# Retention of the second block, two heads at a time: score products alternate between the halves of the array's rows

## The chip, the cores and the metric

The kernel runs on one core of one Trainium2 chip. The metric is device time in microseconds (us), the median of several runs of the whole program. The engines are TensorE (PE, with its weight loads as PEld), VectorE (DVE), ScalarE (ACT), GpSimd (POOL) and the queues that issue DMAs.

## The reference

One sequence of 512 tokens with 1024 features goes through two blocks. The first is a mixer (an mLSTM and a dilated attention) and sixteen routed experts. The second prepends 16 meta tokens (528 tokens in all) and has two layers, each with a mixer and a feed-forward part. The change concerns the retention heads of that second mixer:

```python
RET_HEADS, RET_DK, RET_DV = 4, 48, 96
D_MIX = RET_W + POOL_W + FOX_W               # 384 + 256 + 384
for l in range(DEPTH_2):                     # two layers
    h = hybrid_layer(h, ...)

def hybrid_layer(h, ...):
    q_r, k_r, v_r, g_r, u_p, q_f, k_f, v_f, f_logit = split(h @ w_in)
    qr, kr = rotary(q_r), rotary(k_r)
    o_r = retention(qr, kr, vr)              # o[i] = sum over j <= i of gamma**(i-j) (q_i . k_j) v_j, per head
    o_r = silu(g_r) * head_group_norm(o_r, ret_gn_g)
    o_p = multiscale_pool(u_p)               # trailing means over 2, 4, 8, 16 tokens
    o_f = forgetting_attention(q_f, k_f, v_f, log_sigmoid(f_logit + b_f))   # 6 heads of 64, causal
    h = layer_norm(ALPHA * h + concat(o_r, o_p, o_f) @ w_out)
    return layer_norm(ALPHA * h + (silu(h @ w1) * (h @ w3)) @ w2)
```

## The kernel before

Features stand on partitions and tokens along the free dimension. A dense product in float32 is done as three products of exact 12-bit parts (lines 1377 to 1379, and 1618 to 1620 for the values). Dense work is a stream of jobs, `S`: a call `S.step(us)` emits about that much of it (by its own cost numbers), and `S.until(key)` emits until that job is done. A scheduler then orders the emitted instructions for each engine: an instruction whose inputs or buffers are not there yet is passed by others that were emitted after it.

In the mixer of the second block (`mixer`, from line 1524) the units of retention, attention and pooling are generators. The main loop (line 1918) runs in rounds. In each round every active generator is advanced once, with a `step()` of 1.2 us of dense work behind each of them and one more at the end. `_pipe` starts one unit a round and advances all those that are live. Retention is active from the first round, attention (three pairs of heads, a unit for each of four query tiles, and two tail units for the last 16 tokens) joins after round 4, pooling after round 14. The output projection `wout` follows on the stream when it is empty.

`ret_unit(hd, half)` (line 1693) is one head and one part of the queries, tokens 0 to 287 or 288 to 527. Its first stage multiplies keys by queries for each key tile of 128 tokens (`s<-rqk`, line 1706: 48 rows, in rows 0 to 47 of the array for an even head and 64 to 111 for an odd one), and right behind each product DVE multiplies the scores by the decay (`sw<-s,c_gam`, line 1708). The products of the first part are 288, 160 and 32 columns wide and lie in one PSUM bank. Those of the second part are 240 and 240 in one bank, and 240, 144 and 16 in another. The second stage sums values (`o<-sw`, line 1714) and lets ACT square and copy the sums (lines 1718, 1719). The third forms the norm (lines 1722 to 1725) and, for the heads 0 to 2, calls `S.until(14)`, the last job of the gates, applies the gates (line 1731) and writes the operand of `wout`. Eight units a layer run in the order of heads 3, 0, 1, 2.

Buffers that matter here: PSUM tiles of the kind `s` have four banks, `o` two and `d` (dense) two. SBUF work tiles (`wk`: `sw`, `gv`, `gx`, the attention's `lg` and `PT`, and others) share eight slots. `x3` is a fixed place for the sums of head 3, and `gx` holds those of another head over both of its parts.

The attention's `unit` (line 1769) already works on two heads at once, whose score products (`s<-fqk`, line 1777, 64 rows each) lie in different halves of the array's rows and are emitted one behind the other.

Of the kernel before, what the change touches and what calls it, by code (L numbers as in the profile page):

```python
# [13 lines left out]
AF = mybir.ActivationFunctionType  # L14
OP = mybir.AluOpType
# [17 lines left out]
VSUB, PMUL, VAFF = (1, 3, 5, 7), (2, 4, 6), (1, 5)  # feature tiles of the last norm by engine: DVE subtracts, Pool multiplies, DVE shifts  # L33
# [6 lines left out]
# ---------------------------------------------------------------- host layout  # L40

def _fm(w):
    """[K, M] -> [M/128, 128, K/128 * 128]: stationary tiles, input features on partitions."""
    k, m = w.shape
    return np.ascontiguousarray(
        w.reshape(k // 128, 128, m // 128, 128).transpose(2, 1, 0, 3)).reshape(m // 128, 128, k)


def _padcols(w, groups, width):
    """Columns of w taken group by group, each placed at the start of a band of `width`."""  # L50
    out = np.zeros((w.shape[0], len(groups) * width), np.float32)
# [48 lines left out]
def _host(inp):  # L100
# [88 lines left out]
    # tables that depend on shapes alone  # L189
# [45 lines left out]
# ---------------------------------------------------------------- the program  # L235
# [9 lines left out]
class _Job:  # L245
# [11 lines left out]
    def prep(self, whole=True):  # L257
        """the rest of the preparation, or one step of it"""
# [12 lines left out]
class _Stream:  # L271
    """Dense products in the order of their emission. A job is prepared in two steps, the load of its weights
    (for the next `deep` jobs) and their split (`lead` us ahead). Its run yields the tensor engine's time in us, or None
    while it cannot go on; what has to wait for another engine goes to a tail."""
# [5 lines left out]
    def add(self, key, prep, run, cost=5.0, slow=0):  # L280
        """slow: the time between the steps of a preparation that goes along with the jobs before it"""
        self.jobs.append(_Job(key if isinstance(key, list) else [key], prep, run, cost, slow))
# [22 lines left out]
    def tail(self, g, job=None):  # L305
        """goes on with the steps of g, each after as much time as the one before it yields"""
# [16 lines left out]
    def _one(self):  # L323
        """emits one piece, returns its cost in us"""
# [30 lines left out]
    def until(self, key, flush=False):  # L355
        """goes on until the job is done; flush: its tails at once"""
# [13 lines left out]
    def weave(self, g, first, us):  # L370
        """the rest of the jobs, a step of g after each `us`"""
# [7 lines left out]
def _pipe(units):  # L379
    """the stages of the units, one behind the other"""  # L380
# [12 lines left out]
class _K:  # L393
# [16 lines left out]
    # -- exact split of float32 into two parts of 12 bits  # L410
    def split_w(self, w, n, at=None):
        """w: [128, n] SBUF -> (hi, lo); at: pool, tag, columns and slots"""
# [9 lines left out]
    def after(self, ins, prev):  # L422
        """ins goes behind prev on their engine"""
# [8 lines left out]
    # -- whole program  # L432
# [38 lines left out]
    # -- helpers of the first block  # L471
    def rsqrt(self, r, x, scale, eps, c=1.0, tmp=None):
        """r = c * (scale * x + eps) ** -0.5, the engine's value with one step of Newton's method; r may not be x"""
# [14 lines left out]
    # -- first block, up to the residual after the mixer  # L488
    def first_mixer(self, ctx, mid, keep):
# [32 lines left out]
        # modulation rows: four partial sums side by side, each over a quarter of a half of the features  # L522
# [42 lines left out]
        # first norm  # L565
# [17 lines left out]
        # projections: gates, recurrent input, output gate, then queries, keys and values of the attention  # L583
# [5 lines left out]
        def dense(m, ev, *a):  # L589
# [22 lines left out]
            # the first tile in two parts: the second half of the input is complete later  # L612
# [72 lines left out]
        def ev_qk(ps, i, n):  # L685
# [11 lines left out]
            # queries of a tile stand in reverse, so that their relative positions run up along the partitions  # L697
# [33 lines left out]
        # relative position terms  # L731
# [45 lines left out]
        # modulated input  # L777
# [11 lines left out]
        # recurrent mixer, both directions in quadratic form; units of one head and one query tile  # L789
# [13 lines left out]
        def rec_unit(g, t):  # L803
# [8 lines left out]
            # forward key tiles 0..t, then backward key tiles t..3  # L812
# [58 lines left out]
        # dilated attention: one softmax over the union of the patterns, each key counted as often as it occurs  # L871
# [92 lines left out]
        def square(m, r):  # L964
            """second norm, once the tokens are complete; the router's products are taken before it"""
# [7 lines left out]
            if m == 7:  # L973
                # logits with the tokens on partitions
# [64 lines left out]
        # output projection and residual by halves of the tokens; second norm and router go along  # L1039
# [4 lines left out]
    # -- expert choice  # L1044
    def router(self, ctx):
# [23 lines left out]
        # tokens on partitions, for the gather  # L1069
# [7 lines left out]
        # the largest 64 of each expert, eight at a time  # L1077
# [9 lines left out]
        # slots from 1 on, 0 for a token that the expert leaves out; tokens on partitions, then experts on partitions  # L1087
# [16 lines left out]
    # -- routed experts  # L1104
# [3 lines left out]
    def experts(self, ctx):  # L1108
# [6 lines left out]
        # weights come in pieces of 1 MB; two of them first take places that other tiles need later  # L1115
# [17 lines left out]
        def hold():  # L1133
            """what stands in the two places later on: results and gates of two experts; sums, inputs of two experts"""
# [5 lines left out]
        def gather(p, c):  # L1140
            """inputs of experts 2p and 2p + 1, as exact one-hot products; half c of the features"""
# [56 lines left out]
        def down_last(hds, gu, og):  # L1198
            """features 256 c to 256 c + 255 of the last expert, which complete h; the statistics of the norm that follows"""
# [48 lines left out]
        def onehot(e):  # L1248
            """gate weight of each token at the slot that it has with the expert"""
# [27 lines left out]
        # downward products follow one step behind; those of the last expert come after all of its upward ones  # L1277
# [24 lines left out]
    # -- second block: tokens are the 16 meta tokens and the 512 of the sequence; dense products go by halves  # L1302
# [64 lines left out]
    def mmh(self, ps, r, ks, X, order=None, part=None, cut=None):  # L1367
        """ps[:, 0:n] = W^T x for the tokens r; ks: (split piece, column tile in it, k, rows). Yields its cost in us.
        order: the k-tiles that are ready, in the order of their use. part: first or second part of the sum, cut: its range."""
# [12 lines left out]
    def mmk(self, pss, r, ws, X):  # L1382
        """the same for several column tiles at once, each feature tile of x for all of them before the next one"""
# [17 lines left out]
    def stat(self, k, r):  # L1401
        """running sums over feature tiles of h and of its square"""
# [20 lines left out]
    def norm(self, g, b, r, X, keep=True):  # L1423
        """layer norm of the tokens r of h, in steps; keep: also in the place of h"""
# [42 lines left out]
    def pair(self, ws, n=1024, at=None):  # L1467
        """loads and splits one or two weight tiles of n columns"""
# [5 lines left out]
    def halves_of(self, name, l, R, ws, n, run, cost, at={}, head=None):  # L1474
        """jobs for the eight feature tiles by pairs, first for one half of the tokens, then for the other half, which
        begins with the weights that are still there; head: job for the first three tiles of the first half"""
# [24 lines left out]
    def wout(self, l, R, M, order):  # L1501
# [10 lines left out]
        def head(kept):  # L1512
            """the products of the feature tiles of M that are there go ahead of the last ones"""
# [10 lines left out]
    def mixer(self, l, X, ln, RO, mp):  # L1524
# [43 lines left out]
        # operands of the retention heads, rotated; the forget gates ride along in rows 48 to 53 of the first tile  # L1568
# [32 lines left out]
        # values, tokens on partitions, in the place of h  # L1601
# [28 lines left out]
        # output gates of the retention heads  # L1630
# [22 lines left out]
        # multi-scale pooling  # L1653
# [35 lines left out]
        # retention, quadratic form, queries in two parts; the values are centered, so the sums have no mean  # L1689
        cuts = [slice(0, 288), slice(288, L2)]  # L1690
        gx = {}

        def ret_unit(hd, half):
            i, o = divmod(hd, 2)
            o = slice(64 * o, 64 * o + 48)
            q, k = qk[2 * i], qk[2 * i + 1]
            c = cuts[half]
            n = c.stop - c.start
            banks = [[0, 1, 2]] if half == 0 else [[0, 1], [2, 3, 4]]
            sws = {}  # L1700
            for js in banks:
                ps, sw, at = self.sps(), self.wk("sw"), 0
                for j in js:
                    a = max(c.start, 128 * j)
                    w, kp = c.stop - a, nt[j]
                    nc.tensor.matmul(ps[:kp, at:at + w], k[o, tsl[j]], q[o, a:c.stop], start=True, stop=True)
                    sws[j] = sw[:kp, at:at + w]
                    nc.vector.tensor_mul(sws[j], ps[:kp, at:at + w], cst["c_gam"][:kp, hd, a - 128 * j:c.stop - 128 * j])
                    at += w
            yield  # L1710
            po = self.ops()
            for j in sws:
                a = max(c.start, 128 * j) - c.start
                nc.tensor.matmul(po[:96, a:n], VT[:nt[j], j, 96 * hd:96 * hd + 96], sws[j], start=(j == 0), stop=(j == len(sws) - 1))
            if half == 0:
                gx[hd] = x3 if hd == 3 else self.wk("gx")[:, :L2]
            x, v = gx[hd][:96, c], self.wk("gv")[:96, :n]
            nc.scalar.activation(v, po[:96, :n], AF.Square)
# [417 lines left out]
```

## Time and profile before

| what | value |
| --- | --- |
| time, median of 3 runs | 2672.7 us (2671.11 to 2677.9) |
| profiled execution, first to last instruction | 2671.3 us |
| TensorE busy | 2561.6 us (96%) |
| VectorE, ScalarE, GpSimd busy | 1308.1, 849.1, 370.0 us |
| mean granted TensorE clock | 0.982 |

The profiled execution has no time of its own beside its span. The median of the runs is 1.4 us above that span. The first block and the experts take the span up to about 1340 us. The retention of the first layer runs from about 1419 to 1523 us, that of the second layer from about 2074 to 2178 us.

### The profile page before, as it was taken

Reading aid. Unit: us, or ns where it says so; the run is one execution under the profiler, and the core shown is the slowest. Engines: PE = TensorE matmul, PEld = TensorE weight load, DVE = VectorE, ACT = ScalarE, POOL = GpSimd, SP = SyncE. Lnnn points to the kernel's source line nnn. Section 1 sums busy time; section 2 is a strip of 40 time slices with the busy share of each in tenths; the row PEclk is TensorE's granted clock in tenths of the full one; section 3 lists DMA queues with packets and bytes.
Section 4 is the critical chain, followed back from the end, with each engine's and each line's share of the span. In section 5 each row is a group of like instructions: output and inputs, shape, how many; then the busy total and the mean of one; then the engine's idle time right before and its main releaser. Section 6 shows DMA issues by size and latency. Waiting matters only on the chain.

```text
span 2671.3 us, 39752 instructions
## 1 busy us (share of the span) xinstructions
PE 2561.6 (96%) x16400; PEld 1822.5 (68%) x16400; DVE 1308.1 (49%) x2483; ACT 849.1 (32%) x1601; POOL 370.0 (14%) x361
## 2 busy tenths in 40 slices
PE   7999989999999999999989998999999999899997
PEld 4777765333343433333478878999999888899997
DVE  5476750101010110101273568878876447978796
ACT  3455541000001010000133435434443434534344
POOL 0000010000000000000040125112223013511123
PEclk9999989999999999999989999999999999999999
DMA  7522459999999999999922112223332211232332
GB/s 306 192 93 96 166 196 384 420 402 419 419 419 420 420 420 419 420 419 419 379 86 90 45 57 81 93 95 102 105 109 94 88 46 56 95 103 88 102 108 73
DMA packets 104673, 570.93 MB, mean 214 GB/s; under 512 B 11598, under 2 KB 14926, under 8 KB 50988
## 3 DMA queue, kind: packets, MB, share of 16 engines
q1 hardware_dynamic: 101148, 561.45, 53.4%
q10 hardware_dynamic: 3344, 6.94, 0.8%
q8 instruction: 129, 2.11, 0.3%
q14 instruction: 52, 0.43, 0.0%
HBM read 566.19 MB, written 2.16 MB: 213 GB/s over the span
## 4 chain that ended last, share of the span: by engine, by line
PE 82%; DVE 12%; ACT 2%; DMA 2%; issue 1%; POOL 1%; DVEq 0%; ACTq 0%; POOLq 0%
PE gu L1171 18%; PE py L1195 8%; PE d L1377 6%; PE d L1379 6%; PE d L1378 6%; PE s L1985 5%; PE s L1987 5%; PE s L1986 5%; PE sc L1266 3%; PE sc L1154 3%; DVE wlo L416 2%; PE gt L1182 1%; DVE qlo L1462 1%; DMA ring<-in_w 1%; PE d L1618 1%; PE d L1619 1%
## 5 line engine op out<-in xcount | busy, mean ns | idle before, releaser
L416 DVE TENSOR_TENSOR wlo<-ring,whi 128x1024 fp32r<-128x1024 f32 (+2 forms) x253 | 305.3, 1210 | 126.2 <-ACT whi L416 125.7
L416 ACT ACTIVATE whi<-ring 128x1024 fp32r<-128x1024 f32 (+2 forms) x253 | 248.7, 989 | 354.3 <-PE d L1378 130.7
L1186 DVE TENSOR_TENSOR hd<-sg,gt 128x256 f32<-128x256 f32 x64 | 27.0, 422 | 640.9 <-ACT sg L1184 640.9
L1377 PE MATMUL d<-phi,whi 128*128 128x264 f32 (+1 forms) x888 | 254.4, 287 | 10.5 <-DVE h L1399 7.3
L1378 PE MATMUL d<-plo,whi 128*128 128x264 f32 (+1 forms) x888 | 251.0, 283 | 0.2
L1379 PE MATMUL d<-phi,wlo 128*128 128x264 f32 (+1 forms) x888 | 250.6, 282 | 0.0
L1171 PE MATMUL gu<-ew,xin 128*64 128x512 f32 x1008 | 247.8, 595 | 0.0
L1171 PE MATMUL gu<-ew,late 128*64 128x512 f32 x1024 | 247.4, 595 | 0.0
L1195 PE MATMUL py<-ew,hd 128*64 128x512 f32 x960 | 242.3, 599 | 0.0
L1173 ACT ACTIVATE gus<-gu 128x512 f32<-128x512 f32 x64 | 38.2, 597 | 486.5 <-PE gu L1171 486.5
L1171 PEld LDWEIGHTS gu<-ew,late 128*64 128x64 f32 x1024 | 75.2, 137 | 152.5 <-issue 148.2
L1377 PEld LDWEIGHTS d<-phi,whi 128*128 128x128 f32 x888 | 166.7, 188 | 17.8 <-issue 11.9
L1171 PEld LDWEIGHTS gu<-ew,xin 128*64 128x64 f32 x1008 | 81.7, 137 | 140.4 <-issue 128.6
L1378 PEld LDWEIGHTS d<-plo,whi 128*128 128x128 f32 x888 | 167.3, 188 | 1.4 <-DVE plo L430 0.6
L1379 PEld LDWEIGHTS d<-phi,wlo 128*128 128x128 f32 x888 | 167.2, 188 | 0.2 <-issue 0.2
L1377 PE MATMUL d<-qhi,whi 128*128 128x264 f32 (+1 forms) x496 | 151.9, 306 | 2.3 <-ACT qhi L1461 1.8
L1195 PEld LDWEIGHTS py<-ew,hd 128*64 128x64 f32 x960 | 69.9, 136 | 118.4 <-issue 112.4
L1378 PE MATMUL d<-qlo,whi 128*128 128x264 f32 (+1 forms) x496 | 146.8, 296 | 1.5 <-DVE qlo L1462 1.5
L1379 PE MATMUL d<-qhi,wlo 128*128 128x264 f32 (+1 forms) x496 | 146.8, 296 | 0.0
L1225 POOL TENSOR_TENSOR late<-h 128x528 f32<-128x528 f32 x1 | 1.3, 1315 | 946.7 <-ACT late L1223 946.7
L2010 POOL TENSOR_TENSOR ring<-ring 128x512 f32<-128x512 f32 x38 | 59.3, 1560 | 441.9 <-DVE glo L416 425.3
L1377 PEld LDWEIGHTS d<-qhi,whi 128*128 128x128 f32 x496 | 97.8, 197 | 14.1 <-issue 3.9
(492 smaller groups left out, 5950.4 us busy)
## 6 DMA issues: line engine op xcount, KB each, us to landing
ew<-in_wg SPq DMA_DIRECT2D x127, 1024.0 KB, 17.3
ew<-in_wu SPq DMA_DIRECT2D x127, 1024.0 KB, 16.1
ew<-in_wd SPq DMA_DIRECT2D x120, 1024.0 KB, 17.3
ring<-in_w SPq DMA_DIRECT2D x44, 1024.0 KB, 4.9
ring<-in_win SPq DMA_DIRECT2D x22, 1024.0 KB, 4.9
ring<-in_wada SPq DMA_DIRECT2D x21, 1024.0 KB, 6.2
ring<-in_wout SPq DMA_DIRECT2D x16, 1024.0 KB, 5.0
ring<-in_w SPq DMA_DIRECT2D x24, 640.0 KB, 3.9
```

Source lines behind the costliest of these rows:

```text
L416: both = (nc.scalar.activation(hi[:, :n], w, AF.Copy), nc.vector.tensor_sub(lo[:, :n], w, hi[:, :n].bitcast(F32)))
L1154: nc.tensor.matmul(ps[:, j], self.tok[:, t, 128 * k:128 * k + 128], oh[:, t].rearrange("p a b -> p (a b)"), start=(t == 0), stop=(t == 3))
L1171: nc.tensor.matmul(ps[64 * j:64 * j + 64], x, ws[k // 4][j][:, o], start=(k == 0), stop=(k == 7))
L1195: nc.tensor.matmul(py[64 * c:64 * c + 64], hd[:, j], wd[j // 2][:, o:o + 512], start=(n == 0 and j == 0), stop=(n == 3 and j == 3))
L1266: nc.tensor.matmul(ps, ys[e][s, 128 * (k % 4):128 * (k % 4) + 128], ogs[e][s], start=(i == 0), stop=(i == len(es) - 1))
L1377: nc.tensor.matmul(ps[:, :n], a, X[0][:p, k, r], start=(i == 0 and part != 1), stop=False)
L1378: nc.tensor.matmul(ps[:, :n], a, X[1][:p, k, r], start=False, stop=False)
L1379: nc.tensor.matmul(ps[:, :n], b, X[0][:p, k, r], start=False, stop=(i == len(ks) - 1 and part != 0))
L1985: nc.tensor.matmul(ps, a, x[0][:, k], start=(k == 0), stop=False)
L1986: nc.tensor.matmul(ps, a, x[1][:, k], start=False, stop=False)
L1987: nc.tensor.matmul(ps, b, x[0][:, k], start=False, stop=(k == 3))
L2010: nc.gpsimd.tensor_sub(a11, a21, a11)
```

## The change

A unit is now a pair of heads (3 and 2, then 1 and 0) and one part of the queries, so there are four units a layer. For each bank group the score products of the two heads are emitted alternately, each head into a bank of its own, and all of the decay multiplications come behind all the products of the group. The second part of the queries has a yield behind each of its two groups, the value sums have a yield behind each head, and the norms of both heads share the last stage. `gx` is taken anew for each part. The numbers and shapes of the instructions are the same. The rest of the diff takes out comments.

```diff
-        def ret_unit(hd, half):
-            i, o = divmod(hd, 2)
-            o = slice(64 * o, 64 * o + 48)
-            q, k = qk[2 * i], qk[2 * i + 1]
+        def ret_unit(pr, half):
+            q, k = qk[2 * pr], qk[2 * pr + 1]
             c = cuts[half]
             n = c.stop - c.start
-            banks = [[0, 1, 2]] if half == 0 else [[0, 1], [2, 3, 4]]
-            sws = {}
-            for js in banks:
-                ps, sw, at = self.sps(), self.wk("sw"), 0
+            hds = (2 * pr + 1, 2 * pr)
+            sws = {hd: {} for hd in hds}
+            for js in [[0, 1, 2]] if half == 0 else [[0, 1], [2, 3, 4]]:
+                ps, sw, at = [self.sps() for _ in hds], [self.wk("sw") for _ in hds], 0
+                todo = []
                 for j in js:
                     a = max(c.start, 128 * j)
                     w, kp = c.stop - a, nt[j]
-                    nc.tensor.matmul(ps[:kp, at:at + w], k[o, tsl[j]], q[o, a:c.stop], start=True, stop=True)
-                    sws[j] = sw[:kp, at:at + w]
-                    nc.vector.tensor_mul(sws[j], ps[:kp, at:at + w], cst["c_gam"][:kp, hd, a - 128 * j:c.stop - 128 * j])
+                    for hd, p, s_ in zip(hds, ps, sw):
+                        o = slice(64 * (hd % 2), 64 * (hd % 2) + 48)
+                        nc.tensor.matmul(p[:kp, at:at + w], k[o, tsl[j]], q[o, a:c.stop], start=True, stop=True)
+                        sws[hd][j] = s_[:kp, at:at + w]
+                        todo.append((hd, j, p[:kp, at:at + w], cst["c_gam"][:kp, hd, a - 128 * j:c.stop - 128 * j]))
                     at += w
-            yield
-            po = self.ops()
...
+                for hd, j, p, gam in todo:
+                    nc.vector.tensor_mul(sws[hd][j], p, gam)
+                yield
+            xs, vs = {}, {}
+            for hd in hds:
+                po = self.ops()
+                for j in sws[hd]:
+                    a = max(c.start, 128 * j) - c.start
+                    nc.tensor.matmul(po[:96, a:n], VT[:nt[j], j, 96 * hd:96 * hd + 96], sws[hd][j],
+                                     start=(j == 0), stop=(j == len(sws[hd]) - 1))
+                xs[hd] = x3[:, c] if hd == 3 else self.wk("gx")[:, :n]
+                vs[hd] = self.wk("gv")[:96, :n]
+                nc.scalar.activation(vs[hd], po[:96, :n], AF.Square)
+                nc.scalar.activation(xs[hd][:96], po[:96, :n], AF.Copy)
+                yield
+            for hd in hds:
+                v, x = vs[hd], xs[hd]
...
+                if hd < 3:
+                    S.until(14)
...
             yield
@@
-            for hd in (3, 0, 1, 2):
+            for pr in (1, 0):
                 for half in range(2):
-                    yield ret_unit(hd, half)
+                    yield ret_unit(pr, half)
```

## Rows read from the trace of the kernel before

**Rows 1.** The page, part 1: busy time, share and instructions of each engine.

```profile
PE 2561.6 (96%) x16400; PEld 1822.5 (68%) x16400; DVE 1308.1 (49%) x2483; ACT 849.1 (32%) x1601; POOL 370.0 (14%) x361
```

**Rows 2.** Busy time by stage: length, PE, PEld, DVE, ACT, POOL, granted clock, DMA.

```profile
1419.00:1446.00 27.00, 27.00 (x166) 21.70 (x165) 10.65 (x26) 8.21 (x18) 0.00 (x0) 1.00 0.22 79
...
1510.00:1560.00 50.00, 50.00 (x388) 41.27 (x388) 21.45 (x69) 18.13 (x45) 7.25 (x14) 0.93 0.12 43
...
1535.20:1542.00 6.80, 6.80 (x20) 4.37 (x20) 2.86 (x11) 1.89 (x5) 0.92 (x2) 0.50 0.00 0
...
1580.00:1592.00 12.00, 9.28 (x58) 6.81 (x59) 8.53 (x28) 4.84 (x14) 1.93 (x3) 1.00 0.01 1
...
2190.60:2197.40 6.80, 6.80 (x20) 4.41 (x20) 2.75 (x11) 1.89 (x5) 0.91 (x2) 0.50 0.00 0
```

**Rows 3.** Groups by line, 1415 to 1510 us (first layer): busy, mean ns, idle before.

```profile
L1706 PE MATMUL s<-rqk 48*128 48x240 f32 (+5 forms) x64 | 16.4, 347 | 0.0
...
L1714 PE MATMUL o<-sw,h 128*96 128x240 f32 (+5 forms) x64 | 12.2, 321 | 0.0
...
L1708 DVE TENSOR_TENSOR sw<-s,c_gam 128x240 f32<-128x240 f32 (+5 forms) x32 | 10.2, 328 | 12.5 <-PE s L1706 12.4
```

**Rows 4.** Timeline, head 3, first part: start, length, engine, instruction.

```profile
1418.76 0.28 PE L1619 MATMUL d<-wlo,qhi 128*16 128x256 f32 x1
...
1418.87 0.28 PE L1620 MATMUL d<-whi,qlo 128*16 128x256 f32 x1
...
1419.08 0.75 PE L1706 MATMUL s<-rqk 48*128 48x288 f32 x2
...
1419.76 0.39 PE L1377 MATMUL d<-qhi,whi 128*128 128x264 f32 x1
...
1420.53 0.43 DVE L1708 TENSOR_TENSOR sw<-s,c_gam 128x288 f32<-128x288 f32 x1
...
1421.29 0.54 PE L1706 MATMUL s<-rqk 48*128 48x160 f32 x2
...
1421.75 0.39 PE L1379 MATMUL d<-qhi,wlo 128*128 128x264 f32 x1
...
1424.01 0.41 PE L1706 MATMUL s<-rqk 48*128 48x32 f32 x2
...
1424.34 0.51 PE L1714 MATMUL o<-sw,h 128*96 128x160 f32 x2
```

**Rows 5.** Timeline, head 3, second part; below, the layer's last score product.

```profile
1424.78 0.29 PEld L1706 LDWEIGHTS s<-rqk 48*128 48x128 f32 x2 [0.20 <-issue]
1424.78 0.67 PE L1706 MATMUL s<-rqk 48*128 48x240 f32 x2
1425.38 0.24 PEld L1714 LDWEIGHTS o<-sw,h 128*96 128x96 f32 x2 [0.30 <-issue]
...
1501.77 0.21 PE L1706 MATMUL s<-rqk 48*16 48x16 f32 x2
1501.91 0.39 PE L1378 MATMUL d<-qlo,whi 128*128 128x264 f32 x1
```

**Rows 6.** Timeline of PE: the attention's score products, alone and in pairs.

```profile
1466.76 1.13 PE L1777 MATMUL s<-fqk 64*128 64x512 f32 x4
1467.81 0.39 PE L1618 MATMUL d<-whi,qhi 128*128 128x256 f32 x1
...
1478.30 0.91 PE L1777 MATMUL s<-fqk 64*128 64x384 f32 x3
...
1500.30 0.48 PE L1777 MATMUL s<-fqk 64*128 64x128 f32 x2
1500.72 0.39 PE L1377 MATMUL d<-qhi,whi 128*128 128x264 f32 x1
...
1550.25 0.49 PE L1777 MATMUL s<-fqk 64*128 64x128 f32 x4
1550.67 0.39 PE L1377 MATMUL d<-qhi,whi 128*128 128x264 f32 x1
```

More of the change, by code (lines that the diff above doesn't have):

```diff
@@ L1690, in mixer @@
         cuts = [slice(0, 288), slice(288, L2)]
-        gx = {}
-        def ret_unit(hd, half):
-            i, o = divmod(hd, 2)
-            o = slice(64 * o, 64 * o + 48)
-            q, k = qk[2 * i], qk[2 * i + 1]
+        def ret_unit(pr, half):
+            q, k = qk[2 * pr], qk[2 * pr + 1]
             c = cuts[half]
             n = c.stop - c.start
-            banks = [[0, 1, 2]] if half == 0 else [[0, 1], [2, 3, 4]]
-            sws = {}
-            for js in banks:
-                ps, sw, at = self.sps(), self.wk("sw"), 0
+            hds = (2 * pr + 1, 2 * pr)
[3 more added lines that the diff above has]
+                todo = []
                 for j in js:
@@ L1705, in ret_unit @@
                     w, kp = c.stop - a, nt[j]
-                    nc.tensor.matmul(ps[:kp, at:at + w], k[o, tsl[j]], q[o, a:c.stop], start=True, stop=True)
-                    sws[j] = sw[:kp, at:at + w]
-                    nc.vector.tensor_mul(sws[j], ps[:kp, at:at + w], cst["c_gam"][:kp, hd, a - 128 * j:c.stop - 128 * j])
-                    at += w
-            yield
-            po = self.ops()
-            for j in sws:
-                a = max(c.start, 128 * j) - c.start
-                nc.tensor.matmul(po[:96, a:n], VT[:nt[j], j, 96 * hd:96 * hd + 96], sws[j], start=(j == 0), stop=(j == len(sws) - 1))
@@ L1715, in ret_unit @@
[L1715 to L1718, printed above, removed]
-            nc.scalar.activation(x, po[:96, :n], AF.Copy)
-            yield
-            pm = self.sps()[:96, :n]
-            nc.tensor.matmul(pm, ones[:96, :96], v, start=True, stop=True)
-            nc.scalar.activation(v, pm, AF.Ln, bias=self.eps5[:96], scale=1.0 / 96)
-            nc.scalar.activation(v, v, AF.Exp, scale=-0.5)
@@ L1725, in ret_unit @@
-            nc.vector.tensor_mul(x, x, v)
-            if hd < 3:
-                S.until(14)
-                x = gx[hd][:, c]
-                nc.vector.tensor_copy(x[96:], x3[32 * hd:32 * hd + 32, c])
-                nc.vector.scalar_tensor_tensor(x, x, self.col(f"gn{l}", hd), graw[hd][:, c], op0=OP.mult, op1=OP.mult)
-                self.split_x(M[0][:, hd, c], M[1][:, hd, c], x)
-                if half:
-                    order.append(hd)
+                    for hd, p, s_ in zip(hds, ps, sw):
[3 more added lines that the diff above has]
+                        todo.append((hd, j, p[:kp, at:at + w], cst["c_gam"][:kp, hd, a - 128 * j:c.stop - 128 * j]))
@@ new lines, in ret_unit @@
+            for hd in hds:
+                v, x = vs[hd], xs[hd]
+                pm = self.sps()[:96, :n]
+                nc.tensor.matmul(pm, ones[:96, :96], v, start=True, stop=True)
+                nc.scalar.activation(v, pm, AF.Ln, bias=self.eps5[:96], scale=1.0 / 96)
+                nc.scalar.activation(v, v, AF.Exp, scale=-0.5)
+                nc.vector.tensor_mul(x[:96], x[:96], v)
+                if hd < 3:
+                    S.until(14)
+                    nc.vector.tensor_copy(x[96:], x3[32 * hd:32 * hd + 32, c])
+                    nc.vector.scalar_tensor_tensor(x, x, self.col(f"gn{l}", hd), graw[hd][:, c], op0=OP.mult, op1=OP.mult)
+                    self.split_x(M[0][:, hd, c], M[1][:, hd, c], x)
+                    if half:
+                        order.append(hd)
```

## Prediction

> **What bounds the kernel now.** I read the page first: TensorE is busy for 2561.6 of 2671.3 us, no other engine for half of the span [rows 1]. That is an average, so I read the busy time by stage over the two mixers that the change touches. In the stretch of the first retention units TensorE is busy for 27.00 of 27.00 us and VectorE for 10.65. From 1510 to 1560 it is 50.00 of 50.00 and 21.45 [rows 2]. Whenever a product of retention or attention has to wait, dense products fill TensorE. Only at the very end of the mixer, from 1580 to 1592 us, does TensorE idle, for 2.7 of 12 us [rows 2]. So TensorE time taken out of the retention shortens the mixer by as much, as long as dense work is left to fill the waits, and a wait that delays retention or attention costs nothing until that end.
>
> Then I read the groups by line for what the retention takes of TensorE: the score products of a layer 16.4 us in 64 records (32 products, each two records), the value sums 12.2 us, and the decay multiplications 10.2 us of VectorE [rows 3]. Last, the timeline for what one score product costs from its start to the start of the next instruction. In that stretch the products are spread among dense ones, in 27 runs of one or two adjacent products, from 1419.08 to 1501.77 us [rows 4, 5].
>
> **Why they are spread.** The first product of 288 columns starts at 1419.08, its multiplication on VectorE at 1420.53, and the second product, into the same bank, only at 1421.29, after that multiplication has read [rows 4]. In between stand dense products. The change emits all products of a group before any multiplication, so this wait is gone and the products of a group can stand side by side.
>
> **The price of the score products before.** The 288 columns take 1419.08 to 1419.76, 0.68 us; the 160 columns 0.46; the 32 columns 0.33 [rows 4]. The difference of the first two is 1.7 ns a column, and about 0.2 us remains that a run pays once for getting in and out. A product of 240 columns alone takes 1424.78 to 1425.38, 0.60 us, which agrees, and one of 16 takes 0.14 [rows 5]. For a layer: a record overlaps the next instruction by 0.07 us (0.75 of length against 0.68), 27 runs have 1.9 us of that, so 16.4 - 1.9 = 14.5 us [rows 3, 4]. Besides, dense products start 0.11 us apart, but the first score product starts 0.21 after the dense one ahead of it [rows 4]: 0.10 us for each of the 14 runs that follow a dense product (counted in the timeline).
>
> **The price of a pair.** The trace of before doesn't show a retention pair, but it shows the same thing in the attention. One product of 128 columns of one head alone takes 1500.30 to 1500.72, 0.42 us. Two adjacent ones, of both heads in opposite row halves, take 1550.25 to 1550.67, also 0.42 us. A pair of 512 columns takes 1.05 us [rows 6], which by 0.2 us and 1.7 ns a column is the price of a single one. So an adjacent pair costs as much as one product.
>
> The bounds for a layer, for two pairs of heads. (a) Each pair of products pays the full single price: first part 0.68 + 0.46 + 0.33 = 1.47; second part 3 x 0.60 + 0.44 (144 columns at 0.2 + 1.7 ns each) + 0.14 = 2.38; together 3.85, twice is 7.7 us. (b) The pairs of a group also follow each other without loss, 0.2 us once a group: 480, 480 and 400 columns give 1.0 + 1.0 + 0.9 = 2.9, twice is 5.8 us. (c) No overlap at all, only clusters: 960, 960 and 800 columns, 1.8 + 1.8 + 1.55, twice is 10.3 us. (d) The scheduler tears every pair apart: 14.5 us as now.
>
> I take (a). What speaks against (b) is the weight loads: a product has two, and the two loads of a product of 240 columns take 0.29 us [rows 5], so two heads at once want about 0.5 us of loads for 0.40 us of columns, and more for the narrow products.
>
> The Trainium skill, "TensorE: Matmul & The Clock Gate", section "LDWEIGHTS (loading the stationary operand)", says that a load's time goes by its columns and not by its rows, columns divided by 1.2 in ns. The trace agrees in kind: two loads of 48 rows and 128 columns take 0.29 us [rows 5]. By that page a load is 107 ns (an estimate), so twelve loads, eight, and eight with four short ones make 1.3, 0.9 and 0.9 us, with the 0.2 us of each group 3.7 us a pair of heads and 7.4 us a layer. The saving by the page would be 0.3 us a layer more than by (a).
>
> **The sum.** Score products: 14.5 - 7.7 = 6.8 us a layer, 13.6 us for both. Runs: six a layer in place of 27, so at most 6 entries from dense work for 14, 8 x 0.10 = 0.8 us, 1.6 us for both. Together 15.2 us. The other edits I cost at nothing. The multiplications are the same 32 a layer, later by up to six products. They and the value sums behind them are covered by dense work (10.65 of 27 us busy on VectorE, rows 2). The value sums keep their columns, and their runs of three or five stay. No DMA is added or moved past another. The call of `S.until(14)` comes in round 4 in place of 5, and retention ends two rounds earlier, so two steps of 1.2 us of dense work fall behind. But attention calls for `S.until(5)` and `S.until(6)` and pooling for job 10 in the same rounds as before, and from round 15 on the two programs have emitted the same. If the dense cover were gone, each group's wait from products to value sums (about 2.2 us, six multiplications of 0.33 [rows 3]) would show: six groups a layer, 13 us. The other extreme for these edits is no loss, and I take that since TensorE has no idle stretch between 1419 and 1560 in which the cover fails [rows 2].
>
> From the profiled span, 2671.3 - 15.2 = 2656.1 us. The median of the runs shown is 1.4 us above that span, so the predicted time is 2657.5 us.
>
> **Rivals.**
> 1. *The pairs don't overlap.* The heads have 48 rows and not the attention's 64, and the scheduler may put one head's products first when only one bank is free. By (c) 4.2 us a layer is saved, with the entries 10.0 us in all: 2662.7 us. By (d) there is no gain: 2672.7. For it: the attention's two 128-column products did get torn apart once, at 1500.30, where the run has two records and not four. Against it: the pairs at 1466.76 and 1550.25 [rows 6]. Chance 0.13.
> 2. *The eight work slots make the attention late* (the other side). A retention unit now holds two `sw` for each group, two `gv` and up to two `gx`. By my count of the stages, round 5 asks for thirteen slots with the attention's two `lg`, where eight exist. VectorE and ACT then wait for slots, and behind their waiting instructions stand the attention's softmax and the weight splits. TensorE goes on with dense work, so the delay shows only at the end of the mixer, where dense work is used up and TensorE now idles 2.7 us [rows 2]. A delay that isn't caught up costs its own length. It decides from 7.6 us a layer, the whole gain. Two attention units start at 1466.76 and 1478.30 [rows 6], a round of 11.5 us, so that is two thirds of one round; a whole round in each layer would give 2657.5 + 23 = 2680 us. Against it: a slot is freed by a short chain (multiplication, sum, copy, some 2 us), so I expect delays of that size, caught up later. Chance of a partial loss of 3 to 7 us a layer (2664 to 2672 us) 0.13, of a slower kernel 0.07.
> 3. *The clock moves with the stages.* From 1535.2 to 1542 and from 2190.6 to 2197.4 us the granted clock is 0.50, the lower level of 1.2 GHz [rows 2], each time after a tail unit's run of narrow products. That costs 3.4 us of full speed twice. I keep both in the sum. The stages move by 7 us in the first layer and 15 in the second, and either stretch can vanish or another appear. If both vanish the time is 2651 us. Chance 0.12 for that side; a further stretch of the kind, 2661 us, lies inside the forecast's own range.
>
> **How the numbers follow.** The forecast (pairs overlap, 5.8 to 8.5 us a layer, 2652 to 2663 us with a clock stretch either way) has 0.55; rival 1 0.13, rival 2 0.20, rival 3 0.12. About 0.3%, 8 us, is what a measurement of this kernel can tell from no change. Faster (below 2664.7): the forecast, rival 3, most of rival 1 and a little of rival 2, 0.77. Same: 0.15. Slower: 0.08. The range 2647 to 2670 us takes in (b) with both clock stretches gone at its lower end (2 x 2.8 us and 6.8 us less would be 2646 to 2647), and at its upper end partial losses. It leaves out the torn pairs and a late attention, and holds 8 in 10.
>
> **What the changed profile would show.** The score products' group still has 64 records a layer, but six to ten runs in place of 27, and its busy time falls from 16.4 to about 8 us. If it is near 10.5 us in six runs, the pairs don't overlap; if there are still some twenty runs, they are torn. The multiplications stand behind a whole group. VectorE's waits for score products change their form, not TensorE's. If TensorE's idle time at the end of the mixer grows beyond 2.7 us by several us, the attention is late. The granted clock after the tail unit shows the third rival. The prediction is wrong if the mixer isn't bound by TensorE once the score products are paired: then the busy time falls as told and the span doesn't.

## The result, and the profile after

The kernel after takes 2643.05 us (median of 4 runs, 2639.86 to 2645.13), the kernel before beside it 2674.51 us (4 runs, 2671.11 to 2677.9). The ratio is 0.988, with a 95% interval of 0.9869 to 0.9892: 31.5 us less. I had forecast 2657.5 us and a range from 2647 to 2670. The sign was right; the time lies below the range, and the gain is about twice the 15.2 us of my sum. The profiled execution of after spans 2642.1 us, and its own time is 1.8 us above its span.

The page, part 1, after, answers to [rows 1]: TensorE has lost 29.2 us of busy time in the same 16400 instructions, as much as the spans differ by. Its weight loads have lost 14.0 us, and no other engine has changed by more than 3 us.

```profile
PE 2532.4 (96%) x16400; PEld 1808.5 (68%) x16400; DVE 1305.6 (49%) x2483; ACT 849.7 (32%) x1601; POOL 370.6 (14%) x361
```

The busy time by stage after (length, PE, PEld, DVE, ACT, POOL, granted clock, DMA) answers to [rows 2]. The first stretch begins with the first score product, the second covers later units of the attention, the third follows the tail unit's narrow products, the last is the mixer's end.

```profile
1422.60:1449.60 27.00, 27.00 (x222) 25.51 (x222) 12.10 (x31) 8.41 (x18) 0.00 (x0) 1.00 0.23 79
...
1495.00:1545.00 50.00, 49.92 (x420) 41.08 (x419) 29.56 (x102) 22.50 (x60) 8.83 (x16) 1.00 0.20 72
...
1523.60:1530.40 6.80, 6.80 (x60) 5.61 (x60) 4.29 (x13) 3.49 (x8) 2.38 (x4) 1.00 0.01 2
...
1566.00:1578.00 12.00, 9.16 (x60) 6.69 (x59) 8.60 (x27) 3.77 (x14) 2.62 (x3) 1.00 0.01 1
```

In its first 27 us TensorE is as full as before, and gets 222 records through in place of 166. At the mixer's end it idles 2.84 of 12 us, where it idled 2.72. Behind the tail unit the clock is 1.00, where [rows 2] have 0.50.

The groups by line after, 1418 to 1500 us, answer to [rows 3]; the fourth line is the weight loads of the score products.

```profile
L1719 PE MATMUL o<-sw,h 128*96 128x240 f32 (+5 forms) x64 | 12.5, 322 | 0.0
...
L1712 DVE TENSOR_TENSOR sw<-s,c_gam 128x240 f32<-128x240 f32 (+5 forms) x32 | 8.3, 321 | 11.4 <-PE o L1719 6.1 <-PE s L1707 5.2
...
L1707 PE MATMUL s<-rqk 48*128 48x240 f32 (+5 forms) x64 | 6.6, 329 | 0.0
L1707 PEld LDWEIGHTS s<-rqk 48*128 48x128 f32 (+1 forms) x64 | 4.9, 174 | 1.0 <-issue 0.2
```

The same group of weight loads in the kernel before, 1415 to 1510 us:

```profile
L1706 PEld LDWEIGHTS s<-rqk 48*128 48x128 f32 (+1 forms) x64 | 9.1, 173 | 3.7 <-issue 1.0 <-DVE sw L1708 0.5
```

A score record still lasts about as long (329 ns, before 347), but 64 of them are busy for 6.6 us in place of 16.4: two run at a time. The same holds for the loads: 174 ns each as before, 64 of them in 4.9 us in place of 9.1.

The timeline of PE after, with rows that answer to [rows 4 to 6]:

```profile
1422.59 1.17 PE L1707 MATMUL s<-rqk 48*128 48x288 f32 x12
1423.69 0.39 PE L1377 MATMUL d<-qhi,whi 128*128 128x264 f32 x1
1423.92 0.28 PE L1378 MATMUL d<-qlo,whi 128*128 128x264 f32 x1
...
1432.67 2.17 PE L1707 MATMUL s<-rqk 48*128 48x240 f32 x24
1434.77 0.39 PE L1377 MATMUL d<-qhi,whi 128*128 128x264 f32 x1
1434.99 0.29 PE L1378 MATMUL d<-qlo,whi 128*128 128x264 f32 x1
1435.12 0.29 PE L1379 MATMUL d<-qhi,wlo 128*128 128x264 f32 x1
...
1490.90 0.92 PE L1783 MATMUL s<-fqk 64*128 64x384 f32 x4
1491.74 0.43 PE L1812 MATMUL o<-PT,h 128*64 128x128 f32 x2
...
1501.55 0.49 PE L1783 MATMUL s<-fqk 64*128 64x128 f32 x4
1501.97 0.39 PE L1379 MATMUL d<-qhi,wlo 128*128 128x264 f32 x1
```

The six products of a first part (960 columns of both heads) take 1422.59 to 1423.69, 1.10 us. The twelve of two groups go through in one run, 1432.67 to 1434.77, 2.10 us. A layer has five such runs (1.10, 1.01, 2.10, 1.01 and 1.00 us, 6.2 in all) in place of 27. The first dense product behind a run also takes longer than the next: 1434.77 to 1434.99, 0.22 us, against 0.13 for the one after it. So leaving the dense stream costs 0.10 us [rows 4] and coming back costs about 0.1 us again. The attention's 128-column pair, torn before (2 records at 1500.30 in [rows 6]), stands together here (4 records).

The attention's 384-column pair was not torn before, though [rows 6] show 3 records: that view ends at 1479 us, and the fourth record starts at 1479.01. The same place in the kernel before, 1478 to 1481 us:

```profile
1478.30 1.18 PE L1777 MATMUL s<-fqk 64*128 64x384 f32 x4
1479.42 0.39 PE L1618 MATMUL d<-whi,qhi 128*128 128x256 f32 x1
```

The pair took 1478.30 to 1479.42, 1.12 us, because its second product started 0.28 us after the first; after, it takes 0.84 us. It comes 68.3 us after the first score product, where it came 59.2 us after it.

### The profile page after: what moved, and what is told of

Same layout as the page of the kernel before. It is cut to its first block, busy times and chain, and to the rows that moved or that the text cites. A ratio compares the mean times of both kernels' runs of the same rounds, so it can differ in the third digit from the quotient of the medians.

```text
span 2642.1 us, 39786 instructions
## 1 busy us (share of the span) xinstructions
PE 2532.4 (96%) x16400; PEld 1808.5 (68%) x16400; DVE 1305.6 (49%) x2483; ACT 849.7 (32%) x1601; POOL 370.6 (14%) x361
## 5 line engine op out<-in xcount | busy, mean ns | idle before, releaser
L2016 POOL TENSOR_TENSOR ring<-ring 128x512 f32<-128x512 f32 x38 | 59.2, 1559 | 441.3 <-DVE glo L416 424.8
```

The source lines that it names most:

```text
L2016: nc.gpsimd.tensor_sub(a11, a21, a11)
```

## The experiments

Each differs from after, or from before where that is said, by the edit shown. The times are medians of 4 runs unless another number stands there, the ratios are to the kernel before on the same chip (2674.2 us beside the first four, 2674.3 beside the next three, 2674.5 beside after, so times of different chips can be compared).

**Both heads of a pair in the same half of the rows.** The pairs are heads 3 and 1, then 2 and 0; the planned order stays the same.

```diff
-            hds = (2 * pr + 1, 2 * pr)
+            hds = (2 + pr, pr)
...
                     for hd, p, s_ in zip(hds, ps, sw):
+                        q, k = qk[2 * (hd // 2)], qk[2 * (hd // 2) + 1]
```

> The changed kernel with other pairs: heads 3 and 1, then 2 and 0, so that both heads of a unit lie in the same half of the array's rows; the planned order of the tensor engine is the same row by row. If the gain of the score products is overlap of the two row halves, a layer's score products rise from 6.2 us (five runs, profile of the changed kernel) to about 10.3 us (960, 960 and 800 columns one after the other, five or six runs), and the time from 2643 to about 2651 us. If the products only had to stand together and the rest of the gain is the new staging, the score products' stretch and the time stay, 2643 us.

Measured: 2657.71 us (2657.03 to 2658.63), ratio 0.9941 (0.9926 to 0.9956), 14.7 us more than after. By line, 1410 to 1512 us, score products and their weight loads, and its longest score run with a stretch of the windows that begins in the run's last microsecond:

```profile
L1707 PE MATMUL s<-rqk 48*128 48x240 f32 (+5 forms) x64 | 11.8, 327 | 0.0
...
L1707 PEld LDWEIGHTS s<-rqk 48*128 48x128 f32 (+1 forms) x64 | 9.6, 180 | 1.5 <-issue 0.2
```

```profile
1429.61 4.11 PE L1707 MATMUL s<-rqk 48*128 48x240 f32 x24
```

```profile
1432.96:1436.37 3.41, 3.41 (x17) 3.35 (x17) 0.79 (x3) 0.00 (x0) 0.00 (x0) 0.51 0.00 0
```

The score products take 11.4 us a layer, again in five runs (2.07, 1.81, 4.04, 1.81, 1.69), in place of 6.2: 10.4 us for both layers. The mean granted clock of its runs is 0.9822 against 0.9835 for after, worth 3.4 us: the low stretch at 1433 us begins at the end of the 4 us run, in both layers. 10.4 and 3.4 make 13.8 of the 14.7. The weight loads are busy for 9.6 us in place of 4.9. So the row halves do overlap, products and loads, and what clustering alone saves is 14.46 - 11.42 = 3.0 us of scores a layer.

**Head by head in a group.** The products of one head come first, then those of the other; its plan has them in that order on TensorE.

```diff
-                for j in js:
-                    a = max(c.start, 128 * j)
-                    w, kp = c.stop - a, nt[j]
-                    for hd, p, s_ in zip(hds, ps, sw):
+                for hd, p, s_ in zip(hds, ps, sw):
+                    at = 0
+                    for j in js:
+                        a = max(c.start, 128 * j)
+                        w, kp = c.stop - a, nt[j]
```

> The changed kernel with the products of one head ahead of those of the other in each group, so that they don't alternate; heads still in opposite halves. If products overlap only with a neighbour in the other half, only the last of one head and the first of the other do: about 1.75, 1.4 and 1.5 us for the three groups, 9.3 us a layer in place of 6.2, and 2649 us. If the engine looked further ahead, or if standing together is all that counts, 6.2 us and 2643 us stay.

Measured: 2651.01 us (2649.93 to 2656.25), ratio 0.9919 (0.9903 to 0.9936). By line, 1410 to 1512 us, and the timeline of the groups of a first part and of the first half of a second part:

```profile
L1708 PE MATMUL s<-rqk 48*128 48x240 f32 (+5 forms) x64 | 9.7, 329 | 0.0
```

```profile
1418.31 1.76 PE L1708 MATMUL s<-rqk 48*128 48x288 f32 x12
1420.00 0.39 PE L1377 MATMUL d<-qhi,whi 128*128 128x264 f32 x1
...
1423.99 1.09 PE L1708 MATMUL s<-rqk 48*128 48x240 f32 x8
1425.00 0.39 PE L1377 MATMUL d<-qhi,whi 128*128 128x264 f32 x1
```

The total is as expected, 9.35 us a layer, and 8.0 us over after (6.3 from the scores). How it comes about is not. The group of 240 and 240 columns for each head takes 1.01 us, no more than alternating, though its order is one head, then the other. A start in that order would put the second head's first product beside the first head's second, and the whole at 0.2 + 3 x 0.41 = 1.4 us (an estimate). The eight records start in four twos, the two of each 0.02 us apart or less. The group of 288, 160 and 32 takes 1.69, with the second head beginning beside the first head's second product, and the group of 240, 144 and 16 columns (whose last weights have 16 columns) does not overlap at all: 2 x 0.98. So alternating matters, 3.1 us a layer, but not for every group.

**Multiplications behind the products, single heads.** Kernel before, with one edit: a bank's multiplications come behind all of its products.

```diff
+                    todo.append((j, ps[:kp, at:at + w], cst["c_gam"][:kp, hd, a - 128 * j:c.stop - 128 * j]))
-                    nc.vector.tensor_mul(sws[j], ps[:kp, at:at + w], cst["c_gam"][:kp, hd, a - 128 * j:c.stop - 128 * j])
                     at += w
+                for j, p, gam in todo:
+                    nc.vector.tensor_mul(sws[j], p, gam)
```

> The kernel before, units of one head as they were, with one part of the change alone: the multiplications of a bank come behind all its products. By the price of a run (0.2 us) and 1.7 ns a column the score products of a layer fall from 14.5 to about 11.5 us in 8 to 12 runs, which with fewer entries from dense work gives 7 us: 2667 us. If the new order of emission is most of the gain, it falls well below that, towards 2650 us. A clock stretch more or less is worth 3.4 us.

Measured: 2660.48 us (2658.44 to 2667.17), ratio 0.9955 (0.994 to 0.997): 13.7 us less than before, about twice what I had expected. By line, 1410 to 1512 us:

```profile
L1707 PE MATMUL s<-rqk 48*128 48x240 f32 (+5 forms) x64 | 12.1, 323 | 0.0
```

The score products take 11.55 us a layer in 8 runs, as expected, which gives 5.8 us for both layers. The rest is outside them: the dense products of the first layer stand in 34 runs in place of 48, and by the timeline (from each start to the next) they take 114.0 us in place of 118.3. Of before's 118.3 us, 3.6 lie at the lower clock, and of these 114.0 almost nothing. With such time counted at half it is 114.0 against 116.5, so 14 fewer runs are worth 2.5 us, some 0.2 us each. This was a missing piece in my sum: a score run interrupts the dense stream, and the dense stream pays too.

**Multiplications behind each pair.** After, with the pairs alternating, but each pair's two multiplications right behind it, so that the next pair waits for them as in before.

```diff
-                for hd, j, p, gam in todo:
-                    nc.vector.tensor_mul(sws[hd][j], p, gam)
+                    for hd, jj, p, gam in todo:
+                        nc.vector.tensor_mul(sws[hd][jj], p, gam)
+                    todo = []
```

> The changed kernel with each pair's two multiplications right behind the pair, as the kernel before had them behind each product. The same bank is then read before its next product, as before, so the runs are torn: in the planned order there are about 25 runs a layer, and some pairs stand alone. Priced by runs, about 11 to 12 us of score products a layer and 2653 to 2656 us. If pairing alone, without the later multiplications, carries the gain, 7.7 us a layer (each pair at the price of one product) and 2646 us.

Measured: 2661.73 us (2654.93 to 2664.53), ratio 0.9952 (0.9936 to 0.9968), 18.7 us more than after and more than I had expected. By line, 1410 to 1512 us:

```profile
L1707 PE MATMUL s<-rqk 48*128 48x240 f32 (+5 forms) x64 | 13.2, 356 | 0.2
...
L1707 PEld LDWEIGHTS s<-rqk 48*128 48x128 f32 (+1 forms) x64 | 7.5, 177 | 4.6 <-DVE sw L1712 2.9 <-issue 0.7
```

The wait for `sw` is back on the weight loads (2.9 us), the score products stand in 19 runs and take 11.8 us a layer, and the dense products are back at 48 runs and 118.2 us (114.15 in after). Scores 11.2 us for both layers, and dense runs 2 x 4.0 us, of which up to 1.7 a layer is clock, are 15.8 to 19.2. Seen from before, alternating with this wait left in (and the new staging with it) is 12.4 us faster, the later multiplications on single heads 13.7 us: 26.1 us, where the change with both parts has 31.5. So each part carries a part of the gain, and the two nearly add up.

**Units spread over eleven rounds.** After, with an idle round behind the first pair's second part and behind the second pair's first part, so that retention does not end two rounds earlier.

```diff
                     yield ret_unit(pr, half)
+                    if (pr, half) in ((1, 1), (0, 0)):
+                        yield None
```

> The changed kernel with an empty round behind its second and its third unit, so that retention lasts eleven rounds as before the change in place of nine; the products stay paired except in the last group of a layer, which the planned order tears. The torn group costs 0.7 us a layer and two or three more runs. If the end of retention two rounds earlier is worth nothing by itself, about 2645 us. If the closer staging carries part of the gain that the score products and the clock leave open (some 4 us a layer), up to 2651 us.

Measured: 2658.49 us (2655.64 to 2660.11), ratio 0.9937 (0.9923 to 0.995). Two of four low stretches, behind the tail unit of the first layer and at the mixer's end of the second:

```profile
1522.20:1532.40 10.20, 10.20 (x36) 7.48 (x34) 3.35 (x12) 2.25 (x7) 1.64 (x3) 0.50 0.00 0
...
2222.00:2232.10 10.10, 9.58 (x35) 6.76 (x36) 3.90 (x17) 3.78 (x11) 1.46 (x2) 0.50 0.00 0
```

Its score products take 7.19 us a layer (seven runs, the last group torn in two), 2 us more for both. The mean granted clock of its runs is 0.9788 against 0.9835, and (0.9835 - 0.9788) x 2650 is 12.5 us. The two make 14.5 of the 15.4 us that it is slower than after. So the earlier end of the retention is worth nothing that shows, apart from where it leaves the clock.

**The tail unit's products set apart, in before and in after.** A foreign edit, the same in both: a yield between the four heads' narrow products of the tail unit's last stage, so that dense work comes between them.

```diff
+                if hh < nh - 1:
+                    yield
```

> The kernel before with one foreign edit: a yield between the heads of the attention's tail unit, so that its narrow products (20 of 16 columns, some 3.1 us in one piece) stand apart with dense products between them. If that piece is what lets the clock fall (0.5 for 6.8 us in both layers of the profile of before), the low stretches behind it are gone and the time falls by up to 6 us, to about 2669 us. If the clock falls for another reason, it falls again, and the time stays or rises by a us or two for the added runs.

Measured in before: 2669.15 us (11 runs, 2665.43 to 2674.18), ratio 0.9983 (0.9974 to 0.9991), 5.1 us less. The stretches in which [rows 2] show 0.50:

```profile
1536.00:1545.00 9.00, 9.00 (x85) 7.37 (x84) 3.94 (x13) 2.76 (x7) 1.19 (x3) 1.00 0.36 117
2188.00:2197.00 9.00, 9.00 (x84) 7.34 (x83) 3.98 (x13) 2.71 (x7) 1.22 (x3) 1.00 0.35 118
```

The clock is 1.00 there, and the mean over the runs is 0.9835 (before 0.9811).

> The same edit in the changed kernel, whose profile shows no low stretch there. If the changed kernel's place in time decides whether the clock falls, and it seldom falls in this kernel, nothing is gained: 2643 to 2645 us. If the clock falls in some executions of this kernel too (its runs spread from 2639.9 to 2645.1 us), the spread narrows and the median goes to about 2641 us.

Measured in after: 2641.62 us (2641.05 to 2644.52), ratio 0.9878 (0.9863 to 0.9893). This is the lowest time of all, but its interval overlaps that of after (0.9869 to 0.9892), so the two can't be told apart. Its mean clock is 0.9858. With the tail unit apart in both, the change is worth 2669.15 - 2641.62 = 27.5 us. The mean clocks of the two still differ by 0.0023 (0.9835 and 0.9858), so this difference has a part from the clock too.

**Both kernels once more, unchanged,** for the clock in another execution.

> The kernel before once more, for a second profile of it. If the clock falls behind the tail unit's narrow products whenever this kernel runs, it falls again in both layers (6.8 us at 0.50 each). If it depends on when the piece comes in an execution, it may stand at 1.00 there, and the time is then 2668 to 2671 us and not 2671 to 2678.

> The changed kernel once more. If it is free of the low stretch for a reason of its own, the clock stays at 1.00 behind the tail unit; if it was the place in time of the one profiled execution, it may fall here, in one layer or both, with 3.4 us for each. The score products stay 6.2 us a layer in five runs.

Measured: before 2673.08 us (span 2671.4), after 2645.53 us (span 2643.7). The windows of before again, then of after again, behind the tail unit of each layer:

```profile
1535.00:1541.80 6.80, 6.80 (x20) 4.41 (x21) 2.73 (x11) 1.89 (x5) 0.91 (x2) 0.50 0.00 0
2190.40:2197.10 6.70, 6.70 (x19) 4.31 (x20) 2.75 (x11) 1.90 (x5) 0.91 (x2) 0.50 0.00 0
```

```profile
1517.90:1524.60 6.70, 6.70 (x29) 5.22 (x28) 3.17 (x12) 2.15 (x6) 1.66 (x3) 0.50 0.01 2
2159.60:2166.30 6.70, 6.70 (x31) 5.22 (x32) 2.54 (x10) 1.81 (x5) 1.64 (x3) 0.50 0.00 0
```

The same kernel after, with the same narrow products, falls to the lower level in this execution and not in the one profiled first. So after again has the stretch in both layers, as the first execution of before has in [rows 2], and the two mixers can be compared at the same clock. (Before again has one low stretch more, 3.4 us from 1425.8 us on.)

## Why the prediction was wrong

**What held.** TensorE sets the time, and what is taken out of it there shortens the span. The windows of the whole stage, from the first score product to the mixer's end: before, after, and after again.

```profile
1419.00:1609.20 190.20, 186.52 (x1347) 155.50 (x1346) 100.10 (x270) 75.06 (x177) 33.03 (x48) 0.98 0.20 67
```

```profile
1422.60:1596.60 174.00, 170.92 (x1346) 147.87 (x1346) 98.35 (x270) 75.16 (x177) 33.30 (x48) 1.00 0.21 73
```

```profile
1417.30:1594.30 177.00, 173.88 (x1346) 150.16 (x1346) 98.31 (x270) 75.18 (x177) 33.66 (x48) 0.98 0.21 72
```

The stage loses 16.2 us, or 13.2 us with the low clock as before, and TensorE's busy time loses nearly as much. Pairs cost like one product, the multiplications' later place and the work slots cost nothing that shows, and the waits stay covered: TensorE idles for 3.1 us of the stage after, 3.7 before.

I summed each kind of instruction on TensorE over this stage of the first layer, each from its start to the next start (idle time counts with the instruction ahead of it):

| us, in so many runs | before | after | after again |
| --- | --- | --- | --- |
| dense products | 118.31 in 48 | 114.15 in 38 | 115.45 in 38 |
| retention's score products | 14.46 in 27 | 6.21 in 5 | 6.22 in 5 |
| attention's score products | 15.79 in 19 | 12.81 in 17 | 13.54 in 17 |
| value sums | 11.48 in 10 | 11.04 in 10 | 11.04 in 10 |
| transposes | 9.24 | 8.72 | 9.58 |
| all others | 20.86 | 21.09 | 21.23 |
| sum | 190.14 | 174.02 | 177.06 |
| of it at the lower clock | 6.83 | 0 | 6.83 |

The low stretch falls on dense and attention products in before and on transposes too in after again, and idle time hides in the rows. So here are both layers together, with idle time by itself and time at the lower clock counted at half (an estimate; by it the two executions of before agree within 0.1 us in their sum, those of after within 0.8):

| us, both layers | before | after | after again |
| --- | --- | --- | --- |
| retention's score products | 28.9 | 12.4 | 12.4 |
| dense products (95, 76, 76 runs) | 226.4 | 223.3 | 222.9 |
| attention's score products | 29.1 | 26.2 | 26.1 |
| value sums | 23.0 | 22.1 | 22.1 |
| transposes | 18.3 | 17.3 | 17.1 |
| all others | 40.3 | 40.7 | 40.5 |
| idle | 6.7 | 5.3 | 5.4 |
| sum | 372.7 | 347.4 | 346.6 |

So the mechanism held, and the terms of the sum were too small or missing.

**The step that failed first: the price of a pair, "I take (a)".** I chose (a), 7.7 us a layer, against (b), 5.8 us, because of the weight loads. The layer takes 6.2 us, the 1.0 us a group of (b), the first group 1.1. The loads of two row halves run at the same time (9.1 us busy became 4.9, same length each, and 9.6 with both heads in one half), so the reason against (b) was false. The term was 13.6 us for both layers and measured 16.5.

The figure that I had worked out from the Trainium skill's page "TensorE: Matmul & The Clock Gate", section "LDWEIGHTS (loading the stationary operand)", 7.4 us a layer, fails in the same way: it adds the loads up one behind the other, and the measured 6.2 us is less.

**The second step: the runs, "8 x 0.10 = 0.8 us".** The count of runs was nearly right (five where I said six, and only the first of them follows a dense product), but I priced only the way out of the dense stream. The way back costs as much, and every score run splits a dense run: in the first layer 48 runs became 38, in both 95 became 76. The term was 1.6 us for both layers, and the dense products lost 3.1 to 3.5 us, nearly 0.2 us for each run that is gone. Undoing the order alone (multiplications behind each pair) brings all 48 runs back.

**What I left out: the attention's own pairs, and small terms.** The attention's score products lose 2.9 to 3.0 us in both layers. In the first layer three pairs make it up, 1.4 us, and the second repeats it: the 384-column pair at 1478.30 (1.12 us became 0.84), the 128-column pair (two times 0.41 became 0.42), and a later 384-column pair, 116 us after the first score product. That one stood in two runs within the low stretch, and after it stands in one:

```profile
1535.25 1.64 PE L1777 MATMUL s<-fqk 64*128 64x384 f32 x2
...
1537.55 1.65 PE L1777 MATMUL s<-fqk 64*128 64x384 f32 x2
```

```profile
1524.54 0.92 PE L1783 MATMUL s<-fqk 64*128 64x384 f32 x4
```

That the first two gain because the retention no longer takes score banks in between is my reading of the timeline; no run isolates it. For the third it can't be: the layer's last retention score product lies 33 us ahead of it. With the tail unit set apart in both kernels only the first two are left, 0.7 us a layer. It is not the place of the multiplications: with those behind each pair the attention keeps its 17 runs. Value sums, transposes and idle time, which have no term in my sum, lose 0.9, 1.0 to 1.2 and 1.3 to 1.4 us.

**The sum at equal clock.** Scores 16.5, dense runs 3.1 to 3.5, attention 2.9 to 3.0, the small terms 3.3 to 3.4, less 0.2 to 0.4 for all others: the two mixers are 25.3 to 26.1 us shorter. I had 15.2. From the first score product to the end, before takes 1252.2 us and after again 1226.5, 25.7 us less. (Of it 1.7 us is a low stretch between the layers that only before has.)

**The clock, rival 3.** I kept both low stretches in the sum and gave their vanishing a chance of 0.12. They are no property of the kernel alone: before shows both in both executions, after shows none in one and both in the other. The mean granted clock is 0.9812 over the 22 runs of before beside the first seven experiments and 0.9835 over the four of after, and 0.0023 x 2650 is some 6 us. With the 25.7 us that makes about the 31.5 that were measured. So about 6 us of the measured gain is where the clock happens to fall, by a mean and not run by run. Four runs of after don't tell whether that is chance or the change's doing, and no experiment takes it out: with the tail unit set apart in both kernels the difference is 27.5 us, but the mean clocks are again 0.0023 apart. Without that part the time would have been some 2649 us, just inside my range, with the same terms of the sum too small.

**A slip in the range.** For its lower end I wrote 2 x 2.8 us for (b) in place of (a). By my own prices that is 2 x 1.9 us (7.7 less 5.8), and only with 1.9 do 2646 to 2647 us come out.

**Rival 1 (no overlap)** fell: without overlap the score products take 11.4 us a layer, not 6.2. **Rival 2 (attention late)** happened and cost nothing: the second attention unit is 9 us late, the next ones catch up, and TensorE's idle time at the mixer's end is 2.84 us, before 2.72. No run tried the slots by themselves.

**What stays open:** what decides, in one execution, whether the clock falls behind the tail unit, and whether it falls less often in after; and why the attention's pairs stand together more often.

## What to carry to other kernels

When a small product is put into a stream of dense ones, price the interruption on both sides, about 0.2 us for each run of the dense stream here, and count the runs of the dense stream too. Two heads in opposite halves of the rows can cost TensorE the columns of one, loads included, if nothing on another engine has to answer between their products. Before crediting or debiting a stretch of low clock to an edit, look at a second execution of the same kernel. And when a view shows fewer records than expected, look past the end of its window.

## What the runs showed of the hardware

The weight loads of the two row halves overlap: 64 loads of about 174 ns were busy for 4.9 us, and 64 of about 180 ns for 9.6 us with both heads in the same half. By the planned order, a product of the other half does not always wait behind one that stands ahead of it: two and two products of 240 columns, head by head, took 1.01 us, as long as alternating, and with 16-column weights at the end of a head's products they did not overlap at all (2 x 0.98 us).

The Trainium skill, "TensorE: Matmul & The Clock Gate", section "Part 3: Packing small matmuls — row/col tiling", says that products start and end in program order. The group that took 1.01 us does not agree, if its order on the chip is the planned one; by the page's rule it would be 1.4 us (an estimate). No run here shows that order by itself.

The lower clock level can follow a run of narrow or same-half products: 0.51 from the end of the 4.11 us run on, in both layers of its one execution, and 0.50 for 6.8 us behind the tail unit's narrow products, in some executions and not in others. With dense products between the narrow ones the stretch behind them was gone in the execution profiled, and the mean clock of 11 runs rose from 0.9811 (15 runs of before) to 0.9835.
